# Weight and activation tiles moved to starts on multiples of 128 bytes or more, 260-column weight units in halves

## The chip, the cores and the metric

The kernel runs on one core of a Trainium2 chip, in one launch. The metric is device time in microseconds (us), the median of the runs timed; lower is better. TensorE (PE) does the matmuls, VectorE (DVE) and ScalarE (ACT) the elementwise work, GpSimd (POOL) a few powers and products, and SyncE (SP) issues the transfers. Each of the 128 partitions of the on-chip memory (SBUF) is a row of bytes; a tile takes the same stretch of bytes in every partition, and "address" below means the byte in that row at which a tile or a slice begins.

## The reference, cut to what matters

Two layers on 256 tokens of width 1024, all in float32. `D_FF` is 2816.

```
for l in range(2):
    x = x + 0.5 * swiglu(rmsnorm(x), ffn1_w_in[l], ffn1_w_out[l])
    h = rmsnorm(x)
    x = x + (hybrid_ab_mixer(h) if l == 0 else pool_mixer(h))
    x = x + 0.5 * swiglu(rmsnorm(x), ffn2_w_in[l], ffn2_w_out[l])
return rmsnorm(x)

swiglu(h, w_in, w_out):  gate, up = split(h @ w_in);  (silu(gate) * up) @ w_out
hybrid_ab_mixer(h):      q, k, v, z, b, a, su, sv = split(h @ w_in)
                         # convolution and gated delta rule on q, k, v; gate z; spatial gating of su by sv
                         concat([o_a, o_b]) @ w_out
```

## The kernel before, in words

**Matmuls in three products.** To keep float32 accuracy at the matmul rate of the float32r type, every weight and activation is split into a rounded part `hi` and a remainder `lo`, both float32r. One product of 128 rows then takes three matmuls: hi by hi, hi by lo, lo by hi. Each matmul has a stationary operand of 128 columns, loaded into the array beforehand, and a moving operand whose columns are streamed through it. There are two forms:

- `products_t` (lines 286 to 288): the weights are stationary, the activations of all 256 tokens move. So run the input projections of the FFNs ("pair" units: gate and up for 128 channels; moving `xth`, `xtl`), the q, k and v projections, the output projections of l0a and l0b ("outt" units; moving `hh`, `hl`), and the mixer's output projection (moving `sgh`, `sgl`, `dnh`, `dnl`).
- `products` (lines 278 to 281) and `some` in `out_by_token` (line 437): the activations are stationary, and 512 columns of weights (260 for two units) move from `hi` and `lo`. So run the output projections of l1a and l1b, the first chunk of l1b, and sv, su, ba and z of the mixer; with 256 columns the pool mixer.

**Weights.** They lie packed in one array in the order of use, as units of up to 2080 columns per partition. `load_next` takes a buffer `raw` (3 of them), issues the unit's transfer on SP's queue, and splits it in two halves: ACT writes `hi`, DVE writes `lo` (4 buffers each). `take` hands out the next unit and first calls `load_next` so that loading stays 2 units ahead (1 in the mixer, where a 512-column projection is two units of 4 blocks and a 260-column projection, ba or z, one unit of 8 blocks at a pitch of 260). Within an engine the order of the instructions is fixed when the kernel is built; a planner may put ready work of one part between that of another.

**Where the tiles lie.** A pool lays its tiles one behind the other in order of first use, in multiples of 32 bytes. In the pool `base` these are, with their bytes per partition:

```
xth 8192, xtl 8192, prm 512, xt 8192, ident 512, ones 512, mhalf 64, junk 1024,
raw 3 x 8320, hi 4 x 8320, lo 4 x 8320, sq 2 x 1024, ms 2 x 64, r 2 x 64, rd 1024, rb 2 x 1024, rp 2 x 64, ss 2 x 64
```

The memory map of the built kernel puts `xth` at byte 16512, which is 129 x 128. So `xth`, `xtl` and all up to `mhalf` begin on multiples of 128. `mhalf` takes 64 bytes, and `junk`, `raw`, `hi` and `lo` (8320 is 65 x 128) begin 64 bytes past a multiple of 128. The pools of the stages follow `base`. In the four FFN pools `hh` and `hl` (22528 bytes each) are the first tiles and begin 64 bytes past a multiple of 128 too. In the mixer's pool small tiles of 32 and 64 bytes come first; there `sgh` begins 96 past a multiple of 128, `sgl` on one, `dnh` 96 and `dnl` 32 past one.

`WIDE` (line 27) is the columns of a weight buffer, `LINE` (line 26) those of a small statistics tile. `wide` (line 621) hands out one of two buffers of 4 x 259 values that the mixer uses in turn.

Of the kernel before, what the change touches and what calls it, by code (L numbers as in the profile page):

```python
# [9 lines left out]
F32 = mybir.dt.float32  # L10
F32R = mybir.dt.float32r
# [4 lines left out]
P = 128  # L16
D = 1024
KD = D // P
T = 256
DFF = 2816  # L20
NF = DFF // P
H = 4
# [3 lines left out]
LINE = 16  # L26
WIDE = 130 * LINE
# [26 lines left out]
def weight_units():  # L54

    units = []

    def ffn(name):
        f0 = 0
        if name in FIRST_BY_TOKEN:  # L60
            f0 = 4
            for part in ("g", "u"):
                for h in range(2):
                    units.append((name, "chunk", h, part, 4 * 512))
        for f in range(f0, NF):
            units.append((name, "pair", f, "", 2 * KD * P))
        if name in BY_CHANNEL:
            for d in range(KD):
                for h in range(2):
                    units.append((name, "outt", d, h, NF // 2 * P))  # L70
        else:
            for u in range(NF // 2):
                units.append((name, "out", u, "", 2 * D))

    ffn("l0a")
    for n, w in MIX_CHUNKS:
        halves = 2 if w == 512 else 1
        for h in range(halves):
            units.append(("mix", "in", n, h, KD // halves * w))
    for u in range(4):  # L80
        units.append(("mix", "out", u, "", 2 * D))
    ffn("l0b")
    ffn("l1a")
    units.append(("pool", "w", 0, "", 8 * 256))
    ffn("l1b")
    return units
# [90 lines left out]
def trunk(ctx: ExitStack, tc: tile.TileContext, x_in, xt_in, wts, prm_in, ident_in, mixc_in, band_in,  # L177
          sgw_in, sgn_in, pscale_in, fin_in, out):
    nc = tc.nc
    pe, dve, act, pool = nc.tensor, nc.vector, nc.scalar, nc.gpsimd  # L180

    base = ctx.enter_context(tc.tile_pool(name="base", bufs=1))
    ps = ctx.enter_context(tc.tile_pool(name="ps", bufs=1, space=PSUM))
# [17 lines left out]
    ones = base.tile([P, P], F32, name="ones")  # L201
    pool.memset(ones, 1.0)
    mhalf = base.tile([P, 16], F32, name="mhalf")
# [16 lines left out]
    units = weight_units()  # L220
# [4 lines left out]
    def load_next():  # L225
        u = len(loaded)
        name, kind, _, _, n = units[u]
        raw = base.tile([P, WIDE], F32, tag="raw", name="raw", bufs=RAW_BUFS)
# [4 lines left out]
        if u == 0:  # L233
            for i in range(4):
                c = slice(i * 512, (i + 1) * 512)
                special["first"](i)
                nc.sync.dma_start(out=raw[:, c], in_=src[:, c])
                split(hi[:, c], lo[:, c], raw[:, c])
            return
# [10 lines left out]
        half = n // 2  # L250
# [56 lines left out]
    class Norm:  # L307
# [15 lines left out]
        def means(self):  # L323
            b = chain(0)
            for t in range(2):
                for s in (self.sum, self.last):
                    pe.matmul(out=b[:, t:t + 1], lhsT=s[:, t * P:(t + 1) * P], rhs=ones[:, 0:1],
                              start=s is self.sum, stop=s is self.last)
            ms = base.tile([P, LINE], F32, tag="ms", name="ms", bufs=2)[:, :2]
            dve.tensor_scalar(out=ms, in0=b[:, :2], scalar1=1.0 / D, scalar2=EPS, op0=ALU.mult, op1=ALU.add)  # L330
            r2 = base.tile([P, LINE], F32, tag="r", name="r", bufs=2)[:, :2]
            power(r2, ms)
            self.r = [r2[:, t:t + 1] for t in range(2)]
            self.r2 = r2
# [178 lines left out]
    def rstd(t):  # L513

        ss = base.tile([P, LINE], F32, tag="ss", name="ss", bufs=2)
# [3 lines left out]
        ms = base.tile([P, LINE], F32, tag="ms", name="ms", bufs=2)[:, 0:1]  # L519
# [3 lines left out]
    with tc.tile_pool(name="pl", bufs=1) as pp:  # L523
# [7 lines left out]
        band_r = pp.tile([P, 4, P + 16], F32, name="band_r")  # L531
        x_tail = pp.tile([P, D], F32, name="x_tail")
        last = Norm()
        last.r2 = base.tile([P, LINE], F32, tag="r", name="r", bufs=2)[:, :2]
        last.r = [last.r2[:, t:t + 1] for t in range(2)]

        def pooled(t):
            r = base.tile([P, LINE], F32, tag="rp", name="rp", bufs=2)[:, 0:1]
# [45 lines left out]
    def final(t):  # L584
        o = fin_pool.tile([P, D], F32, tag="o", name="o", bufs=2)
        halves = [slice(n * 512, (n + 1) * 512) for n in range(2)]
        r = base.tile([P, LINE], F32, tag="rp", name="rp", bufs=2)[:, 0:1]
# [11 lines left out]
def mixer(tc, e):  # L599
# [9 lines left out]
    def load(w):  # L609
        if w == 512:  # L610
            return [blocks_of(take("mix", "in", 1), w, 0, 4) for _ in range(2)]
        return [blocks_of(take("mix", "in", 1), w, 0, KD)]

    with tc.tile_pool(name="mx", bufs=1) as mp:
# [6 lines left out]
        def wide(form="p h t -> p h t"):  # L621
            return mp.tile([P, H, T + 3], F32, tag="wide", name="wide", bufs=2).rearrange(form)
# [3 lines left out]

        mixc, sgn, ws = consts["mixc"], consts["sgn"], consts["sgw"]
# [64 lines left out]
        sv = mp.tile([P, 2, 512], F32, tag="sv", name="sv")  # L692
# [5 lines left out]
        def conv(first):  # L698
            y = mp.tile([P, H, T], F32, name=f"y{first}")
            pre = wide()  # L700
# [23 lines left out]
        def norms(y, at):  # L724

            sq = wide()[:, :, :T]
# [111 lines left out]
        raw_sv, sv = sv, wide("p h t -> p (h t)")[:, :1024].rearrange("p (t c) -> p t c", t=2)  # L838
# [12 lines left out]
        su = wide("p h t -> p (h t)")[:, :1024].rearrange("p (t c) -> p t c", t=2)  # L851
# [24 lines left out]
        sg_parts = (mp.tile([P, 4, 2, P], F32R, tag="sv", name="sgh"), mp.tile([P, 4, 2, P], F32R, name="sgl"))  # L876
# [66 lines left out]
        for u in range(2):  # L943
            w = take("mix", "out", 1)
            for i in range(2):
                for d in range(KD):
                    some(OUT_ORDER[2 * u + i], i, w, d)
        dn_parts = tuple(mp.tile([P, H, T + 3], F32R, tag="wide", name=n, bufs=2).rearrange("p h t -> p (h t)")[:, :1024]
                         .rearrange("p (k t c) -> p k t c", k=4, t=2) for n in ("dnh", "dnl"))
# [40 lines left out]
```

## Time and profile before

| | us |
|---|---|
| median of 3 runs | 917.57 |
| lowest and highest | 914.7, 920.32 |
| the profiled execution's own time | 916.53 |
| its span, first to last instruction | 914.7 |

The profile is of one execution. A line of a view names the line of the kernel, the engine, the operation and the tiles as out<-in. A matmul's duration in it covers its passage through the array, which overlaps with the next ones; the pace, from one start to the next, is had by counting matmuls in a stretch. A window counts every instruction that touches it, so a stretch of matmuls without a gap has the pace (length of the window + one duration) / count; one duration is 0.28 us for 256 columns and 0.39 us for 512.

### The profile page before, as it was taken

The page shows a single profiled execution, that of the slowest core. Times are in us where ns is not written, and L with a number is a line of the kernel's source. Part 1 is how long each engine was busy: PE and PEld are TensorE (multiplying, and loading weights), DVE is VectorE, ACT ScalarE, POOL GpSimd, SP SyncE. Part 2 cuts the span into 40 slices and gives each one's busy share as a digit, 9 for nine tenths or more (in the row PEclk, how much of TensorE's full clock was granted, in tenths as well). Part 3 has the DMA queues.
Part 4 walks back from the last instruction along what each step waited for, and adds up shares of the span by engine and source line. Part 5 has one row for each costly group of instructions (what it writes and reads, how often), then busy time and mean ns, then how long its engine had stood idle before and what let it go on. Part 6 is the DMA issues. An engine that isn't in the chain of part 4 may idle for free.

```text
span 914.7 us, 16344 instructions
## 1 busy us (share of the span) xinstructions
PE 897.9 (98%) x6900; PEld 855.1 (93%) x6900; DVE 573.6 (63%) x907; ACT 456.9 (50%) x717; POOL 28.9 (3%) x40
## 2 busy tenths in 40 slices
PE   8999999999999999999999999999999999999996
PEld 7999999999988989999999999999888789999885
DVE  5866656667887676666556666566555566666443
ACT  6655534466647565544444545455335445544331
POOL 0000000000221000000000000000000000000000
PEclk9999999999999999999999999999999899999999
DMA  7865545663224235555455765555555165555521
GB/s 275 336 197 203 168 130 188 218 232 136 96 92 164 72 136 216 198 185 174 153 165 201 265 232 205 172 201 195 184 186 182 48 231 192 199 184 188 193 81 47
DMA packets 25851, 162.86 MB, mean 178 GB/s; under 512 B 2993, under 2 KB 3121, under 8 KB 9649
## 3 DMA queue, kind: packets, MB, share of 16 engines
q1 hardware_dynamic: 25488, 161.29, 51.0%
q8 instruction: 54, 0.88, 0.4%
q10 hardware_dynamic: 288, 0.52, 0.1%
q14 instruction: 21, 0.16, 0.0%
HBM read 160.75 MB, written 1.05 MB: 177 GB/s over the span
## 4 chain that ended last, share of the span: by engine, by line
PE 94%; DVE 3%; ACT 1%; DMA 1%; issue 0%; SPq 0%; POOL 0%; POOLq 0%; ACTq 0%; DVEq 0%
PE mm L286 18%; PE mm L288 18%; PE mm L287 18%; PE acc L437 13%; PE acc L288 5%; PE acc L286 5%; PE acc L287 5%; PE mm L278 2%; PE mm L279 2%; PE mm L281 2%; DMA xt<-in_xt 1%; PE acc L556 1%; PE acc L799 0%; PE acc L793 0%; PE acc L271 0%
## 5 line engine op out<-in xcount | busy, mean ns | idle before, releaser
L213 ACT CAST hi<-raw 128x1024 fp32r<-128x1024 f32 (+2 forms) x318 | 307.0, 986 | 331.7 <-PE mm L287 204.0
L214 DVE TENSOR_TENSOR lo<-raw,hi 128x1024 fp32r<-128x1024 f32 (+2 forms) x318 | 360.7, 1151 | 125.9 <-ACT hi L213 125.4
L286 PE MATMUL mm<-xth,hi 128*128 128x256 f32 x1440 | 400.9, 279 | 0.5 <-ACT xth L216 0.5
L287 PE MATMUL mm<-xtl,hi 128*128 128x256 f32 x1440 | 399.9, 278 | 0.5 <-DVE xtl L217 0.4
L288 PE MATMUL mm<-xth,lo 128*128 128x256 f32 x1440 | 399.1, 277 | 0.8 <-DVE lo L214 0.8
L286 PEld LDWEIGHTS mm<-xth,hi 128*128 128x128 f32 x1440 | 271.0, 188 | 1.5 <-ACT xth L216 0.9
L287 PEld LDWEIGHTS mm<-xtl,hi 128*128 128x128 f32 x1440 | 271.3, 188 | 1.0 <-DVE xtl L217 0.9
L288 PEld LDWEIGHTS mm<-xth,lo 128*128 128x128 f32 x1440 | 271.0, 188 | 1.2 <-DVE lo L214 1.2
L405 DVE TENSOR_TENSOR sg<-mm,rb 128x256 f32<-128x256 f32 x84 | 35.3, 424 | 112.5 <-PE mm L288 112.3
L286 PE MATMUL acc<-hh,hi 128*128 128x256 f32 x352 | 99.3, 282 | 0.0
L288 PE MATMUL acc<-hh,lo 128*128 128x256 f32 x352 | 99.2, 282 | 0.0
L287 PE MATMUL acc<-hl,hi 128*128 128x256 f32 x352 | 99.1, 282 | 0.0
L437 PE MATMUL acc<-hi,hh 128*128 128x512 f32 x176 | 69.3, 394 | 0.0
L437 PE MATMUL acc<-lo,hh 128*128 128x512 f32 x176 | 69.0, 392 | 0.0
L437 PE MATMUL acc<-hi,hl 128*128 128x512 f32 x176 | 69.0, 392 | 0.0
L286 PEld LDWEIGHTS acc<-hh,hi 128*128 128x128 f32 x352 | 66.7, 189 | 0.0
L288 PEld LDWEIGHTS acc<-hh,lo 128*128 128x128 f32 x352 | 66.6, 189 | 0.0
L287 PEld LDWEIGHTS acc<-hl,hi 128*128 128x128 f32 x352 | 66.6, 189 | 0.0
L213 ACT CAST hh<-hid 128x256 fp32r<-128x256 f32 x84 | 34.0, 408 | 27.8 <-DVE hid L408 27.7
L437 PEld LDWEIGHTS acc<-hi,hl 128*128 128x128 f32 x176 | 33.0, 188 | 7.7
L437 PEld LDWEIGHTS acc<-hi,hh 128*128 128x128 f32 x176 | 33.0, 188 | 7.5
L437 PEld LDWEIGHTS acc<-lo,hh 128*128 128x128 f32 x176 | 33.1, 188 | 7.3
(211 smaller groups left out, 784.9 us busy)
## 6 DMA issues: line engine op xcount, KB each, us to landing
raw<-in_wts SPq DMA_DIRECT2D x124, 1024.0 KB, 4.9
raw<-in_wts SPq DMA_DIRECT2D x32, 704.0 KB, 4.1
raw<-in_wts SPq DMA_DIRECT2D x2, 1040.0 KB, 4.9
xt<-in_xt SPq DMA_DIRECT2D x4, 256.0 KB, 5.7
raw<-in_wts SPq DMA_DIRECT2D x4, 256.0 KB, 5.9
mixc<-in_mixc SPq DMA_DIRECT2D x1, 640.0 KB, 6.3
band<-in_band SPq DMA_DIRECT2D x1, 544.0 KB, 6.4
psc<-in_pscale SPq DMA_DIRECT2D x1, 512.0 KB, 8.2
```

Of the source, the lines that this page charges most:

```text
L213: act.copy(out=hi, in_=src)
L214: dve.tensor_tensor(out=lo, in0=src, in1=hi.bitcast(F32), op=ALU.subtract)
L278: pe.matmul(out=b, lhsT=ah, rhs=wh, start=start and i == 0, stop=False)
L279: pe.matmul(out=b, lhsT=ah, rhs=wl, start=False, stop=False)
L281: pe.matmul(out=b, lhsT=al, rhs=wh, start=False, stop=stop and i == n - 1)
L286: pe.matmul(out=b, lhsT=wh, rhs=ah, start=start, stop=False, **more)
L287: pe.matmul(out=b, lhsT=wh, rhs=al, start=False, stop=False, **more)
L288: pe.matmul(out=b, lhsT=wl, rhs=ah, start=False, stop=stop, **more)
L405: dve.tensor_tensor(out=sg, in0=gate, in1=norm.rb, op=ALU.mult)
L437: pe.matmul(out=acc[t][n], lhsT=a, rhs=w[part][:, n * 512:(n + 1) * 512], start=first and i == 0, stop=last and i == 2)
L556: pe.matmul(out=o, lhsT=x[:, t, c], rhs=band_r[:, g, :P], start=True, stop=True)
```

## The change

The tiles that float32r matmuls read get other addresses. Small statistics tiles are made 128 bytes (`LINE` = 32), `mhalf` and the rows `ms`, `r`, `ss` are set out first in `base` (7 tiles of 128 bytes, so `xth` begins at 16512 + 896 = 17408, which is 17 x 1024), and `WIDE` becomes 2048 columns, 8192 bytes. Two tiles `pad` that nothing uses round up what stands before others. In the mixer, both `wide` buffers (now 4 x 264 values, 33 x 128 bytes), `sv` and `sgl` are set out first. Since a unit of 2080 columns no longer fits, ba and z are packed as two units of 4 blocks, like the 512-column projections; each is loaded by one transfer that puts its 260-column blocks at a pitch of 512 columns, and split in two pieces of two blocks, so that each block begins on a multiple of 2048 bytes. No arithmetic changes.

```diff
-LINE = 16
-WIDE = 130 * LINE
+LINE = 32
+WIDE = 2048
...
     for n, w in MIX_CHUNKS:
-        halves = 2 if w == 512 else 1
-        for h in range(halves):
-            units.append(("mix", "in", n, h, KD // halves * w))
+        for h in range(2):
+            units.append(("mix", "in", n, h, KD // 2 * w))
...
     base = ctx.enter_context(tc.tile_pool(name="base", bufs=1))
+    def row(tag):
+        return base.tile([P, LINE], F32, tag=tag, name=tag, bufs=2)
+    mhalf = base.tile([P, LINE], F32, name="mhalf")
+    for tag in ("ms", "r", "ss"):
+        row(tag)
...
     ones = base.tile([P, P], F32, name="ones")
+    base.tile([P, P], F32, name="pad")
     pool.memset(ones, 1.0)
-    mhalf = base.tile([P, 16], F32, name="mhalf")
...
+        if n == 4 * 260:
+            raw, src, hi, lo = (a.rearrange("p (k c) -> p k c", k=4) for a in (raw, src, hi, lo))
+            nc.sync.dma_start(out=raw[:, :, :260], in_=src)
+            for c in (slice(0, 2), slice(2, 4)):
+                split(hi[:, c, :260], lo[:, c, :260], raw[:, c, :260])
+            return
...
         band_r = pp.tile([P, 4, P + 16], F32, name="band_r")
+        pp.tile([P, P], F32, name="pad")
...
     def load(w):
-        if w == 512:
-            return [blocks_of(take("mix", "in", 1), w, 0, 4) for _ in range(2)]
-        return [blocks_of(take("mix", "in", 1), w, 0, KD)]
+        halves = [blocks_of(take("mix", "in", 1), 512, 0, 4) for _ in range(2)]
+        return [[(wh[:, :w], wl[:, :w]) for wh, wl in half] for half in halves]
...
-        def wide(form="p h t -> p h t"):
-            return mp.tile([P, H, T + 3], F32, tag="wide", name="wide", bufs=2).rearrange(form)
+        def wide(name="wide", dtype=F32):
+            return mp.tile([P, H, T + 8], dtype, tag="wide", name=name, bufs=2)
+        def flat(a):
+            return a.rearrange("p h t -> p (h t)")[:, :1024]
...
+        wides = [wide(), wide()]
+        sv = mp.tile([P, 2, 512], F32, tag="sv", name="sv")
+        sgl = mp.tile([P, 4, 2, P], F32R, name="sgl")
...
-            pre = wide()
+            pre = (wides.pop() if wides else wide())[:, :, :T + 3]
...
-            sq = wide()[:, :, :T]
+            sq = (wides.pop() if wides else wide())[:, :, :T]
...
-        sg_parts = (mp.tile([P, 4, 2, P], F32R, tag="sv", name="sgh"), mp.tile([P, 4, 2, P], F32R, name="sgl"))
+        sg_parts = (mp.tile([P, 4, 2, P], F32R, tag="sv", name="sgh"), sgl)
...
-        dn_parts = tuple(mp.tile([P, H, T + 3], F32R, tag="wide", name=n, bufs=2).rearrange("p h t -> p (h t)")[:, :1024]
-                         .rearrange("p (k t c) -> p k t c", k=4, t=2) for n in ("dnh", "dnl"))
+        dn_parts = tuple(flat(wide(n, F32R)).rearrange("p (k t c) -> p k t c", k=4, t=2) for n in ("dnh", "dnl"))
```

What is left out replaces `base.tile([P, LINE], ...)` by `row(...)` and `wide("p h t -> p (h t)")[:, :1024]` by `flat(wide())`.

## Rows read from the trace of the kernel before

**Rows 1.** The page: busy time of each engine, and its granted clock in 40 slices.

```profile
PE 897.9 (98%) x6900; PEld 855.1 (93%) x6900; DVE 573.6 (63%) x907; ACT 456.9 (50%) x717; POOL 28.9 (3%) x40
...
PEclk9999999999999999999999999999999899999999
```

**Rows 2.** The page: the chain of work that ended last, share of the span by engine.

```profile
PE 94%; DVE 3%; ACT 1%; DMA 1%; issue 0%; SPq 0%; POOL 0%; POOLq 0%; ACTq 0%; DVEq 0%
```

**Rows 3.** Windows, PE alone: stretch and length, busy (matmuls), granted clock, DMA share, GB/s.

```profile
40.00:140.00 100.00, 100.00 (x882) 1.00 0.54 183
155.00:195.00 40.00, 40.00 (x339) 1.00 0.63 215
312.00:318.00 6.00, 6.00 (x53) 1.00 0.01 3
...
360.00:480.00 120.00, 120.00 (x1051) 1.00 0.52 177
...
589.00:593.00 4.00, 4.00 (x36) 1.00 0.46 137
596.00:603.00 7.00, 7.00 (x64) 1.00 0.45 154
645.00:695.00 50.00, 50.00 (x218) 1.00 0.55 190
```

**Rows 4.** Groups by line and shape, PE: how many matmuls of each kind.

```profile
L286 PE MATMUL mm<-xth,hi 128*128 128x256 f32 x1440 | 400.9, 279 | 0.5 <-ACT xth L216 0.5
...
L286 PE MATMUL acc<-hh,hi 128*128 128x256 f32 x352 | 99.3, 282 | 0.0
...
L437 PE MATMUL acc<-hi,hh 128*128 128x512 f32 x176 | 69.3, 394 | 0.0
...
L278 PE MATMUL mm<-hi,xth 128*128 128x512 f32 x64 | 25.9, 405 | 1.0 <-ACT xth L213 1.0
```

**Rows 5.** The chain in order of time: start, length, what and how often.

```profile
205.99 0.93 PE mm L281 x4
...
237.41 1.68 PE acc L732 x16
...
246.03 0.59 DVE wide L711
...
257.25 0.45 PE acc L799 x4
...
277.00 0.96 PE mm L281 x8
...
347.18 0.43 PE acc L341 x2
```

**Rows 6.** Groups by line and shape, ACT: the rounding of weights into hi.

```profile
L213 ACT CAST hi<-raw 128x1040 fp32r<-128x1040 f32 x4 | 4.1, 1061 | 5.7 <-PE mm L287 3.9 <-PE acc L287 1.8
...
L213 ACT CAST hi<-raw 128x512 fp32r<-128x512 f32 x4 | 2.4, 605 | 0.2 <-DMA raw<-in_wts 0.2
```

**Rows 7.** Groups by line and shape, DVE: the remainders of weights into lo.

```profile
L214 DVE TENSOR_TENSOR lo<-raw,hi 128x1040 fp32r<-128x1040 f32 x4 | 5.4, 1367 | 1.7 <-ACT hi L213 1.7
...
L214 DVE TENSOR_TENSOR lo<-raw,hi 128x512 fp32r<-128x512 f32 x4 | 2.8, 692 | 0.4 <-ACT hi L213 0.4
```

**Rows 8.** The page, DMA issues: bytes, and median us from issue to landing.

```profile
raw<-in_wts SPq DMA_DIRECT2D x2, 1040.0 KB, 4.9
...
psc<-in_pscale SPq DMA_DIRECT2D x1, 512.0 KB, 8.2
```

**Rows 9.** Timeline of SP near 175 us: the first of the two is ba's transfer.

```profile
175.05 4.19 SPq L240 DMA_DIRECT2D raw<-in_wts  x2
```

**Rows 10.** Timeline of PE near 196 us: the first matmul of ba.

```profile
195.92 0.28 PE L278 MATMUL mm<-hi,xth 128*128 128x260 f32 x1
```

**Rows 11.** Timeline of PE near 275 us: the first matmul of z.

```profile
274.92 0.28 PE L278 MATMUL mm<-hi,xth 128*128 128x260 f32 x1
```

**Rows 12.** Timeline of ACT in the stage of z.

```profile
273.64 3.90 ACT L213 CAST hi<-raw 128x1024 fp32r<-128x1024 f32 x4 [4.03 <-PE mm L287]
```

More of the change, by code (lines that the diff above doesn't have):

```diff
@@ L328, in means @@
                               start=s is self.sum, stop=s is self.last)
-            ms = base.tile([P, LINE], F32, tag="ms", name="ms", bufs=2)[:, :2]
+            ms = row("ms")[:, :2]
             dve.tensor_scalar(out=ms, in0=b[:, :2], scalar1=1.0 / D, scalar2=EPS, op0=ALU.mult, op1=ALU.add)
-            r2 = base.tile([P, LINE], F32, tag="r", name="r", bufs=2)[:, :2]
+            r2 = row("r")[:, :2]
             power(r2, ms)
@@ L513, in rstd @@
     def rstd(t):
-        ss = base.tile([P, LINE], F32, tag="ss", name="ss", bufs=2)
+        ss = row("ss")
         for n in range(2):
@@ L518, in rstd @@
                            accum_out=ss[:, n:n + 1])
-        ms = base.tile([P, LINE], F32, tag="ms", name="ms", bufs=2)[:, 0:1]
+        ms = row("ms")[:, 0:1]
         dve.tensor_scalar(out=ms, in0=ss[:, 0:1], scalar1=ss[:, 1:2], scalar2=EPS, op0=ALU.add, op1=ALU.add)
@@ L531, in trunk @@
         band_r = pp.tile([P, 4, P + 16], F32, name="band_r")
+        pp.tile([P, P], F32, name="pad")
         x_tail = pp.tile([P, D], F32, name="x_tail")
         last = Norm()
-        last.r2 = base.tile([P, LINE], F32, tag="r", name="r", bufs=2)[:, :2]
+        last.r2 = row("r")[:, :2]
         last.r = [last.r2[:, t:t + 1] for t in range(2)]
         def pooled(t):
-            r = base.tile([P, LINE], F32, tag="rp", name="rp", bufs=2)[:, 0:1]
+            r = row("rp")[:, 0:1]
             power(r, rstd(t))
@@ L586, in final @@
         halves = [slice(n * 512, (n + 1) * 512) for n in range(2)]
-        r = base.tile([P, LINE], F32, tag="rp", name="rp", bufs=2)[:, 0:1]
+        r = row("rp")[:, 0:1]
         power(r, rstd(t))
@@ L689, in mixer @@
             dl.append(c)
-        sv = mp.tile([P, 2, 512], F32, tag="sv", name="sv")
         banks = project(512, load(512), False)
@@ L835, in mixer @@
             act.activation(out=zs[:, t, 252:], in_=banks[t][:, :260], func=AF.Silu, scale=r[t])
-        raw_sv, sv = sv, wide("p h t -> p (h t)")[:, :1024].rearrange("p (t c) -> p t c", t=2)
+        raw_sv, sv = sv, flat(wide()).rearrange("p (t c) -> p t c", t=2)
         act.activation(out=sv, in_=raw_sv, func=AF.Gelu)
@@ L850, in mixer @@
                                          op0=ALU.mult, op1=ALU.mult)
-        su = wide("p h t -> p (h t)")[:, :1024].rearrange("p (t c) -> p t c", t=2)
+        su = flat(wide()).rearrange("p (t c) -> p t c", t=2)
         banks = project(512, load(512), False)
```

## The prediction

> **What bounds the kernel now.** I read the page first. TensorE is busy for 98% of the span and the others for 63% or less [rows 1], and the chain of work that ended last lies on PE for 94% of the time [rows 2]. So the end moves by what a matmul costs, and hardly by what ACT, DVE or the transfers cost. The granted clock is at full speed, 2.4 GHz, in nearly every slice [rows 1] and 1.00 in every stretch used below [rows 3], so the clock explains none of the differences.
>
> Next I read windows that hold nothing but matmuls, and took the pace (window plus one duration, over the count). Matmuls of 256 moving columns come in two paces. In the pair stages, where `xth` and `xtl` move, it is 100.28 / 882 = 113.7 ns and 120.28 / 1051 = 114.4 ns; in the outt stage, where `hh` and `hl` move, 40.28 / 339 = 118.8 ns; in the mixer's output projection 6.28 / 53 = 118.5 ns [rows 3]. Count, shape, clock and stationary operand (`hi` and `lo`, 64 bytes past a multiple of 128) are the same in all three. What differs is the address of the moving operand: on a multiple of 128 for `xth` and `xtl`, 64 past one for `hh` and `hl`, mostly off one in the mixer. With 512 moving columns of `hi` or `lo`, 64 past a multiple, the pace is 50.39 / 218 = 231.1 ns [rows 3], and 0.93 / 4 = 232 ns in the mixer [rows 5]. Twice 113.7 would be 227.4. The last two come with a stationary operand off (L437, `hh`) and on a multiple of 128 (L281, `xtl`), and are alike: for 512 columns the stationary address doesn't tell, the moving one may.
>
> The reading is not clean. Between 589 and 593 us the pair stage itself runs at 4.28 / 36 = 118.9 ns, and between 596 and 603 us, with the same moving tiles, at 7.28 / 64 = 113.8 ns [rows 3]. And in the stretch from 312 us one of three matmuls moves `sgl`, which is on a multiple of 128, yet the whole stretch is at 118.5. So an aligned moving tile can reach 113.7 but need not, and the tiles off a multiple do not reach it in any stretch that I read.
>
> **The change part by part.** After it the float32r tiles, moving and stationary, begin on multiples of 128 bytes (the sizes add up so: 896 bytes of small tiles ahead of `xth`, weight buffers of 8192, `wide` of 4224).
>
> (a) outt: 3 x 352 = 1056 matmuls [rows 4] go from 118.8 to 113.7 ns: 1056 x 5.1 = 5.4 us.
>
> (b) 512 moving columns: 3 x 176 = 528 of L437 and 3 x 64 = 192 of L278 to L281 [rows 4]. The trace has no 512-column float32r matmul on a multiple of 128, so its pace is bounded: at best 0.43 / 2 = 215 ns, which two passes of 256 float32 columns take [rows 5] and which is nearly 512 columns at 2.4 GHz (213 ns); at worst 227 ns, twice the aligned 256. I take the middle, 221: 528 x 10.1 = 5.3 us and 192 x 11 = 2.1 us. The ends give 11.8 and 3.1 us in all in place of 7.4.
>
> (c) 260 columns: 2 projections x 2 token tiles x 8 blocks x 3 = 96 matmuls from 0.96 / 8 = 120 ns [rows 5] to 113.7 x 260 / 256 = 115.5: 0.4 us.
>
> (d) The mixer's output projection (4 units x 2 x 8 x 3 = 192) and the pool mixer's 48: 240 x 5 = 1.2 us.
>
> (e) The pair stages stay at their pace: 0. If the slow stretches in them go as well, about (114.4 - 113.7) ns over 4320 matmuls, 3 us at most.
>
> All of (a) to (d) stand on the path, since PE has no gaps in these stretches: 5.4 + 7.4 + 0.4 + 1.2 = 14.4 us. Faster matmuls ask for weights sooner. A unit of 24 matmuls of 512 columns would last 5.3 us in place of 5.5; its splitting takes about 2 x 1.4 us on DVE [rows 7], and its transfer lands in 4.9 us with three buffers in turn [rows 8]. PE stays the bound.
>
> What the halves of ba and z cost: four casts of 520 columns in place of two of 1040. By the 512-column rows that is 4 x 0.61 - 2 x 1.06 = 0.3 us of ACT and 4 x 0.70 - 2 x 1.37 = 0.1 us of DVE per unit [rows 6, 7], beside PE. Two transfers in runs of 1040 bytes take the place of one in runs of 8320. No row has that form; two halves of one 4.9 us transfer would cost nothing, and two like psc's 8.2 us would land 11.5 us later [rows 8]. ba's transfer starts at 175.05 and its first matmul at 195.92 [rows 9, 10]: 21 us less 4.9 is more than 11.5. I take zero, on either end.
>
> Both projections fill one more of the four `hi` and `lo` buffers, so the unit four places on is split one place later. For su's first half this cover is thin: its buffer comes free with q's last matmul, at about 274.9 [rows 11], z lasts 48 x 120 ns = 5.8 us, and two casts and the last subtraction take 2 x 1.06 + 1.37 = 3.5 us; 2.3 us are spare. ACT does take up casts at once when such buffers come free, four in a row [rows 12]. The price if ACT or DVE is held up elsewhere is up to 3.5 us, there and once more at sv after ba. Behind a waiting cast stand ACT's silu of z and its square of q's convolution, which PE needs only after z. The planner may also mix the mixer's pieces in another order. I take 0.3 us for all of it, bounds -1 and +3.
>
> The swapped turns of `wide`: v's convolution now writes the buffer of k's squares instead of k's inputs. PE has read the squares by 239.1 and DVE writes v's first half at 246.03 [rows 5]; 7 us of cover, zero cost, 7 us later the most that its loss could bring. Longer small rows and pads: zero, they are storage.
>
> Sum: 14.4 - 0.3 = 14.1 us. The profiled execution took 916.53 us, 1.0 below the median, with a span of 914.7; from it, 916.5 - 14.1 = 902.4. I forecast 902. The case's own range, from the ends of (b), (e) and the mixer, is 894 to 909.
>
> **The rivals.**
>
> Slower: the address of the moving operand against that of the weights decides, not either one alone. While one matmul streams, PE loads the weights of the next. In the pair stage the two lie 64 bytes apart modulo 128, and this is the one relation seen at 113.7; in outt both are 64 past, relation zero, and slow. After the change the relation is zero everywhere. Then the pair and q, k, v matmuls, 3 x 1440 = 4320 [rows 4], fall to the outt pace: 4320 x 5.1 = 22.0 us lost, nothing won in (a), 916.5 + 22.0 + 0.3 = 939; with the 7.4 us of (b), 931. It decides from the point at which more than two thirds of the pair matmuls lose their pace. Two pair stretches on the same tiles at two paces speak for some such interplay; against it, the 512-column rows show no gain when the weights are on a multiple and the moving tile 64 past, which is also 64 apart. Chance 0.20.
>
> No change: the start of a tile does not matter, and the 113.7 belongs to `xth` for another reason, or is a phase that the stage falls into by itself (589 to 603 us). Then the time is 916.5 + 0.3 = 917. The Trainium skill speaks for it: "SBUF — State Buffer", section Specifications (TRN2), gives the memory lines of 16 bytes and a penalty for crossing to a new one. By that rule a start 64 bytes past a multiple of 128 is as good as one on it, and the sum is zero. The trace disagrees as far as 118.8 against 113.7 goes. Chance 0.14.
>
> Faster still: the weight loads gain too. Matmuls of 128 float32 columns, whose streams are short, come every 0.45 / 4 = 112.5 ns [rows 5], which I take for the pace that loading 128 weight columns allows. From 113.7 to 112.5 over 4320 + 1056 + 240 matmuls is 6.7 us, and 512 columns at 215 give 4.4 more: 891. Chance 0.10. The Trainium skill, "TensorE: Matmul & The Clock Gate", section Back-to-back issue gap, gives N / 2.4 + 2.5 ns for an isolated matmul: 109.2 and 215.8 ns. No stretch here shows 109.2 for float32r; by an estimate from that page the pair stages alone would give 4320 x 4.5 = 19 us.
>
> **How the numbers follow.** Main case 0.56, slower 0.20, no change 0.14, faster still 0.10. The predicted time is the main case's. Within 1% (908.4 to 926.7; three runs spread over 0.6%, so less is hard to tell from nothing) lie the no-change case and 0.03 of the main one, 0.17. Below lie 0.53 + 0.10 = 0.63, above 0.20. The range 888 to 932 holds the first, third and fourth cases and the milder part of the second; the rest, some 0.15, is left out.
>
> **What would show it.** In the profile after, windows inside outt should hold about 355 matmuls in 40 us in place of 339, windows of L437 about 228 in 50 us in place of 218, pair windows 882 in 100 us as before. If pair windows hold 845, the slower rival is right. If 339 and 218 stay, nothing came of the addresses. If PE shows gaps between 270 and 285 us, the halves cost more than I gave. What would make it wrong most easily is the pair stage: it holds 4320 of the matmuls, it has its pace already, and I cannot show that it keeps it once the weights move too.

## The result, and the profile after

The kernel after takes 942.26 us (median of 6 runs, 938.92 to 945.36), the kernel before 917.79 (6 runs, 914.70 to 920.32). The ratio is 1.0264, 95% interval 1.0232 to 1.0295: slower, where 902 was forecast. Products stand at lines 300 to 302 (`products_t`), 292 to 295 (`products`) and 451 (`out_by_token`) in the kernel after; the splits of weights at 220 and 221.

The page of the kernel after, against [rows 1, 2, 8]: busy times with the granted clock, the chain by engine, and the transfers of the halves (count, KB each, us to landing).

```profile
PE 918.9 (98%) x6900; PEld 879.6 (94%) x6900; DVE 574.0 (61%) x911; ACT 456.7 (49%) x721; POOL 30.0 (3%) x40
...
PEclk9999999999999999999999999999999999999999
...
PE 92%; DVE 4%; ACT 1%; DMA 1%; issue 1%; POOL 1%; SPq 0%; POOLq 0%; ACTq 0%
...
raw<-in_wts SPq DMA_DIRECT2D x4, 520.0 KB, 4.1
```

TensorE (PE) is the bound as before, with the same 6900 matmuls, a granted clock of 0.9 or more in every slice (1.00, that is 2.4 GHz, in every stretch used below), and 21 us more busy time. So each matmul costs more. The windows say which, PE alone (stretch and length, busy with the count, granted clock, DMA share, GB/s), against [rows 3]; the stretches after 195 us are set later, since the stages begin later. l0a, l0b, l1a and l1b are the two FFNs of layer 0 and of layer 1, in order.

```profile
40.00:140.00 100.00, 100.00 (x836) 1.00 0.52 177
155.00:195.00 40.00, 40.00 (x336) 1.00 0.58 184
319.00:325.00 6.00, 6.00 (x52) 1.00 0.01 3
365.00:465.00 100.00, 100.00 (x835) 1.00 0.51 174
...
560.00:650.00 90.00, 90.00 (x754) 1.00 0.51 176
596.00:603.00 7.00, 7.00 (x61) 1.00 0.42 150
665.00:715.00 50.00, 50.00 (x222) 1.00 0.57 193
```

The pace is again (window + one duration) / count. Where a pace is said to be "from start to start", it is the mean step between the starts of neighbouring matmuls in the trace, without gaps. Pairs take 100.28 / 836 = 119.95 ns (before 113.7), 120.1 in l0b (before 114.4) and 119.7 in l1a. The outt stage takes 40.28 / 336 = 119.9 (before 118.8), the mixer's last product 6.28 / 52 = 120.8 (118.5); there one matmul is 2.3 ns, and from start to start it is 119.3 (118.6). The 512-column streams of l1a take 50.39 / 222 = 227.0 (before 231.1). All matmuls of 256 columns have come to one pace, 120 ns; in the trace 5308 of 5529 of them start exactly 120 ns before the next.

The groups by line and shape of the kernel after, against [rows 4, 6, 7], show that the counts are unchanged and what the halves of ba and z cost in splitting.

```profile
L300 PE MATMUL mm<-xth,hi 128*128 128x256 f32 x1440 | 409.6, 285 | 2.5 <-ACT hi L220 1.5 <-ACT xth L223 1.1
...
L451 PE MATMUL acc<-hi,hh 128*128 128x512 f32 x176 | 68.6, 390 | 0.0
...
L220 ACT CAST hi<-raw 128x520 fp32r<-128x520 f32 x8 | 4.6, 625 | 10.0 <-PE mm L301 5.4 <-PE acc L301 4.6
...
L221 DVE TENSOR_TENSOR lo<-raw,hi 128x520 fp32r<-128x520 f32 x8 | 6.4, 825 | 1.3 <-ACT hi L220 1.3
```

ba's two transfers in the timeline of SP, and the first matmuls of ba and of z in that of PE, against [rows 9 to 11]:

```profile
182.16 4.41 SPq L250 DMA_DIRECT2D raw<-in_wts  x2
...
203.21 0.28 PE L292 MATMUL mm<-hi,xth 128*128 128x260 f32 x1
...
281.81 0.28 PE L292 MATMUL mm<-hi,xth 128*128 128x260 f32 x1
```

From ba to z it is 78.6 us, 79.0 before, and from ba to l0b's first matmul 137.2, 137.4 before: the mixer did not get slower by the halves or by the swapped turns of `wide`. The loss lies in the stages that run on `products_t`. By these paces: pairs and q, k, v 4320 x (120.0 - 114.0) = +25.9 us, outt 1056 x 1.1 = +1.2, the mixer's output 192 x 0.8 = +0.1, streams 528 x 4.1 + 192 x 3.5 = -2.8 (L278 to L281 went from 232 to 228.5 from start to start). That is +24.4; the spans differ by 22.4, the medians by 24.5.

### The profile page after: what moved, and what is told of

It is laid out like the page before. It is cut to its first block, busy times and chain, and to the rows that moved or that the text cites. A ratio compares the mean times of both kernels' runs of the same rounds, so it can differ in the third digit from the quotient of the medians.

```text
span 937.1 us, 16363 instructions
## 1 busy us (share of the span) xinstructions
PE 918.9 (98%) x6900; PEld 879.6 (94%) x6900; DVE 574.0 (61%) x911; ACT 456.7 (49%) x721; POOL 30.0 (3%) x40
## 4 chain that ended last, share of the span: by engine, by line
PE 92%; DVE 4%; ACT 1%; DMA 1%; issue 1%; POOL 1%; SPq 0%; POOLq 0%; ACTq 0%
PE mm L300 19%; PE mm L302 19%; PE mm L301 19%; PE acc L451 12%; PE acc L302 5%; PE acc L300 5%; PE acc L301 5%; PE mm L292 2%; PE mm L293 2%; PE mm L295 1%; DVE lo L221 1%; DMA xt<-in_xt 1%; PE acc L571 1%; DVE y L737 0%; ACT hi L220 0%
## 5 line engine op out<-in xcount | busy, mean ns | idle before, releaser
L220 ACT CAST hi<-raw 128x1024 fp32r<-128x1024 f32 (+3 forms) x322 | 307.3, 976 | 357.8 <-PE mm L301 230.4
L221 DVE TENSOR_TENSOR lo<-raw,hi 128x1024 fp32r<-128x1024 f32 (+3 forms) x322 | 360.6, 1137 | 125.7 <-ACT hi L220 125.3
L300 PE MATMUL mm<-xth,hi 128*128 128x256 f32 x1440 | 409.6, 285 | 2.5 <-ACT hi L220 1.5
L302 PE MATMUL mm<-xth,lo 128*128 128x256 f32 x1440 | 408.0, 283 | 1.0 <-DVE lo L221 1.0
L301 PE MATMUL mm<-xtl,hi 128*128 128x256 f32 x1440 | 408.1, 284 | 0.5 <-DVE xtl L224 0.4
L300 PEld LDWEIGHTS mm<-xth,hi 128*128 128x128 f32 x1440 | 276.2, 192 | 3.9 <-ACT hi L220 2.1
L302 PEld LDWEIGHTS mm<-xth,lo 128*128 128x128 f32 x1440 | 276.2, 192 | 1.4 <-DVE lo L221 1.4
L301 PEld LDWEIGHTS mm<-xtl,hi 128*128 128x128 f32 x1440 | 276.2, 192 | 1.0 <-DVE xtl L224 0.9
L419 DVE TENSOR_TENSOR sg<-mm,rb 128x256 f32<-128x256 f32 x84 | 35.4, 424 | 137.4 <-PE mm L302 137.3
```

The source lines that it names most:

```text
L220: act.copy(out=hi, in_=src)
L221: dve.tensor_tensor(out=lo, in0=src, in1=hi.bitcast(F32), op=ALU.subtract)
L300: pe.matmul(out=b, lhsT=wh, rhs=ah, start=start, stop=False, **more)
L301: pe.matmul(out=b, lhsT=wh, rhs=al, start=False, stop=False, **more)
L302: pe.matmul(out=b, lhsT=wl, rhs=ah, start=False, stop=stop, **more)
L419: dve.tensor_tensor(out=sg, in0=gate, in1=norm.rb, op=ALU.mult)
```

## Experiments

The theories of the first four kernels. R: what counts is the distance, modulo 128, of the address of the streamed operand from that of the loaded one; zero is slow for 256 columns. W: the weights' own address; on a multiple of 128 they are slow. M: the streamed operand has to be on a multiple of 128 and the weights off it. S: the halves of ba and z, or the order of the mixer, not the addresses. All edits are to the kernel after, save in the fourth. "Pair", "outt" and "stream" paces below are from windows of PE in the stages of l0a, l0a and l1a.

The ratio is to runs of before that were timed along with each kernel (their medians lie between 916.57 and 918.05 us).

| kernel | weights, activations (mod 128) | us | ratio to before, 95% | pair, outt, stream ns |
|---|---|---|---|---|
| before | 64; 0, hh and hl 64 | 917.79 | | 113.4, 118.8, 231.1 |
| after | 0; 0 | 942.26 | 1.0264 (1.0232 to 1.0295) | 120.1, 119.9, 227.0 |
| e1 | 64; 0 | 918.79 | 1.0005 (0.9981 to 1.0029) | 113.4, 117.6, 233.3 |
| e2 | 0; 64 | 930.84 | 1.0139 (1.0108 to 1.0169) | 117.7, 117.9, 234.4 |
| e3 | 96, 0, 32, 64 in turn; 0 | 928.86, one run | | 117.4, 117.3, 231.1 |
| e4 | as before | 915.63 | 0.9974 (0.9957 to 0.9992) | 113.3, 118.8, 231.1 |
| e8 | 32; 0 | 941.21, one run | | 118.3, 120.1, 234.4 |
| e10 | 64; 64 | 943.46, one run | | 119.9, 119.8, 227.0 |
| e12 | 64; 0, l1's hh and hl 64 | 919.93 | 1.0029 (1.0014 to 1.0044) | 113.3, 117.6, 232.2 |
| e14 | 64, low parts 128 further; 0 | 911.80 | 0.9942 (0.9923 to 0.9961) | 113.4, 113.2, 231.1 |
| e15 | 0, low parts 128 further; 64 | 920.28 | 1.0038 (1.0015 to 1.0062) | 113.4, 113.2, 230.1 |
| e9 | by use (below); 0 | 910.01 | 0.9912 (0.9894 to 0.9931) | 113.3, 113.5, 230.1 |
| e11 | by use, streams 0 mod 256; 0 | 909.16 | 0.9906 (0.9886 to 0.9925) | 113.4, 113.2, 226.0 |
| e13 | as e11, with q, k, v | 908.72 | 0.9906 (0.9882 to 0.9929) | 113.4, 113.2, 226.0 |

The windows: 40 to 130 us for pairs (90.28 over the count), 145 to 190 for outt (45.28), 50 us inside l1a's output projection for the streams (50.39); before's and after's outt and streams are those of the sections above. One matmul more or less in a window is 0.2, 0.3 and 1 ns.

**e1: weights 64 past, activations on multiples.**

```diff
     junk = base.tile([P, 512], mybir.dt.bfloat16, name="junk")
+    base.tile([P, 16], F32, name="shift")
...
         load_next()
+        base.tile([P, 16], F32, name="back")
```

> The changed kernel with all weight buffers (raw, hi, lo) moved 64 bytes up, so that they begin 64 past a multiple of 128 as in the kernel before, while xth, xtl, hh, hl, sgh, sgl, dnh and dnl stay on multiples. Theory R (the moving address against the weights' address modulo 128 decides; 64 apart is fast, zero apart slow): pair and outt stages both at 113.4 ns in place of 120.0, so 4320 x 6.6 + 1056 x 6.6 = 35 us less than the changed kernel: 907, 1.2% below the kernel before. Theory W (the weights' own address decides, 64 past is fast): the same 907, so this run does not tell R from W. Theory S (the halves of ba and z and the new order of the mixer cost the time): 942 as the changed kernel.

918.79 us: 64 bytes ahead of the weight buffers give back the whole loss. Windows of e1, PE: pairs of l0a, outt, pairs of l0b.

```profile
40.00:130.00 90.00, 90.00 (x796) 1.00 0.56 190
145.00:190.00 45.00, 45.00 (x385) 1.00 0.59 188
365.00:445.00 80.00, 80.00 (x708) 1.00 0.54 186
```

Pairs are at 113.4 again, as in before. But outt, with `hh` and `hl` on multiples and the weights 64 past, as R and M want it, stays at 45.28 / 385 = 117.6.

**e2: the reverse, activations 64 past, weights on multiples.**

```diff
+    base.tile([P, 16], F32, name="shift")
     xth = base.tile([P, KD, 2, P], F32R, name="xth")
...
-    base.tile([P, P], F32, name="pad")
+    base.tile([P, P - 16], F32, name="pad")
...
         load_next()
+        base.tile([P, 16], F32, name="shift2")
```

> The mirror image: the weights stay on multiples of 128 as in the changed kernel, and all activations (xth, xtl, hh, hl, sgh, sgl, dnh, dnl) begin 64 past one. Theory R: 64 apart again, pair and outt at 113.4 ns, about 907. Theory W: the weights are on multiples, so pair and outt stay at 120.0: about 942. A third theory, M (a moving operand must be on a multiple and the weights off it), gives 942 as well. For 512 moving columns no theory has a number: 226.7 ns (both on multiples) and 231 (both 64 past) are known.

930.84 us, between the two. Windows of e2: pairs of l0a, and of l1a before 580 us and after 589.

```profile
40.00:130.00 90.00, 90.00 (x767) 1.00 0.55 189
...
553.00:580.00 27.00, 27.00 (x232) 1.00 0.54 193
...
589.00:630.00 41.00, 41.00 (x364) 1.00 0.56 193
```

117.7 ns, 27.28 / 232 = 117.6, and then 41.28 / 364 = 113.4 on the same tiles. W and M fall in their strict form: 113.4 is reached with the weights on multiples and the streamed tiles off them. R stands for the zero distance, but says too little: 64 apart has two paces, 113.3 and about 117.7. The change falls where four transposes by `by_token` stand between pair units, the first at 581.9 us.

**e3: four places in turn.** Weight buffers of 2056 columns, so that units begin 96, 0, 32 and 64 past.

```diff
-WIDE = 2048
+WIDE = 2048 + 8
...
-            raw, src, hi, lo = (a.rearrange("p (k c) -> p k c", k=4) for a in (raw, src, hi, lo))
+            raw, src, hi, lo = (a[:, :w].rearrange("p (k c) -> p k c", k=4) for a, w in ((raw, 2048), (src, n), (hi, 2048), (lo, 2048)))
...
+        base.tile([P, 8], F32, name="back")
```

> The changed kernel with weight buffers at a pitch of 8224 bytes, so that the four of hi, and the four of lo alike, begin 96, 0, 32 and 64 bytes past a multiple of 128, unit by unit in turn; all activations on multiples. Theory R and W: in the pair and outt stages every fourth unit (64) at 113.4 ns and every fourth (0) at 120.0; 32 and 96 are open: as slow as 0 if only 64 is special, in between if the distance counts. If the pace depends on what the stage fell into before, units of one offset will differ among themselves.

Windows of e3 in l0a: the first inside a unit 96 past, the second inside one 64 past, then such a pair once more.

```profile
58.50:63.00 4.50, 4.50 (x41) 1.00 0.48 178
64.20:68.50 4.30, 4.30 (x40) 1.00 0.43 179
81.00:85.50 4.50, 4.50 (x41) 1.00 0.54 180
86.50:91.00 4.50, 4.50 (x42) 1.00 0.45 189
```

4.78 / 41 = 116.6 and 4.58 / 40 = 114.5 by these short windows; from start to start it is 118.2 and 113.3. The units on a multiple or 32 past run at 118 to 119. Only 64 apart shows 113.3.

**e4: before, with the halves of ba and z alone.**

```diff
-        halves = 2 if w == 512 else 1
-        for h in range(halves):
-            units.append(("mix", "in", n, h, KD // halves * w))
+        for h in range(2):
+            units.append(("mix", "in", n, h, KD // 2 * w))
...
+        if n == 4 * 260:
+            raw, src, hi, lo = (a[:, :w].rearrange("p (k c) -> p k c", k=4) for a, w in ((raw, 2048), (src, n), (hi, 2048), (lo, 2048)))
+            nc.sync.dma_start(out=raw[:, :, :260], in_=src)
```

(and in `load`, as in the change.)

> The kernel before with the second part of the change alone: ba and z as two units each at a pitch of 512 columns, all tiles where they were. Theories R and W: 917 to 920, no difference (the mixer was 137.5 us from ba's first matmul to l0b's first in the kernel before and 137.2 in the changed one, with 250 matmuls slowed in it). Theory S: most of the 24.5 us, 935 or more.

915.63 us, 0.9974 of before: S is out, the halves cost nothing and perhaps win 1 to 4 us by the interval. Where, the profiles do not settle: the profiled execution of e4 has a span of 916.0, at a mean granted clock of 0.990 for before's 0.993. From ba to z it took 77.5 us for before's 79.0, but from ba to l0b's first matmul 137.4 as in before.

The next four sharpen R to D: zero apart leaves 120 for 256 columns and gives 227 for 512; 64 apart allows 113.3 and 117.8, one of which goes on until a gap draws again. N is the rival without such a rule.

**e5: placing by use, first try.** Units that are loaded (`products_t`) 64 past, units that are streamed on multiples.

```diff
+        held = kind in ("pair", "outt") or name == "mix" and (kind == "out" or units[u][2] in CONV_CHUNKS)
+        o = 16 * (held ^ u % 2)
-        hi = base.tile([P, WIDE], F32R, tag="hi", name="hi", bufs=SPLIT_BUFS)
+        hi = base.tile([P, WIDE + 16], F32R, tag="hi", name="hi", bufs=SPLIT_BUFS)[:, o:o + WIDE]
```

(`lo` likewise.)

> The kernel after, with each weight unit placed by how it is used: units that are loaded as weights (pairs, outt, k, v, q and the mixer's last product) begin 64 bytes past a multiple of 128, units that are streamed (chunk, out, sv, su, ba, z, pool) on a multiple; the activations stay on multiples. Theory D (the distance of the streamed address from the loaded one modulo 128 sets the pace; zero leaves 256 columns only 120 ns, 64 apart allows 113.3 and 117.8; 512 columns go the other way, zero 227 and 64 apart 232): 702 matmuls of 512 columns go from the 232.3 ns of the kernel with weights 64 past to 227.1, so its 918.8 us less 3.7, 915; and 910.5 if outt (1056 matmuls) draws the faster of its two paces this time, 113.3 for 117.8. So 910 to 916. Rival N (it is the weights' own addresses, or where all buffers stand together, and no rule by use): the times of the kernels with all weights at one place, 918 or more, with outt at 117.8 and the streams at 231 to 233.

919.94 us (ratio 1.0027, 1.0013 to 1.0040), above D's range; the time is within N's, but outt is at 115.4 from start to start and the streams at 229.6, where N has 117.8 and 231 to 233. The kernel was not what it meant to be: the addresses show `hi` and `lo` of one unit in buffers of different number, so that in half of the units one of the two is on the wrong side. The units with both 64 past ran at 113.3 to 113.4 from start to start, in outt too; the other pair units had means of 115 to 118.

**e6: high parts 64 past, low parts on multiples** (`hi` 32 columns longer and begun 16 columns in).

> The kernel after, with the high parts of the weights 64 bytes past a multiple of 128 and the low parts on multiples; activations on multiples. Of each three matmuls the first two have the high part loaded, the third the low part. Theory D with the matmul's own weights: the interval from the third matmul to the next is 120, those from the first two 113 or 118. If it is the weights that are being loaded meanwhile for the next matmul: the interval from the second is 120 and the other two are short. Rival N: all three alike, at 120 or at a mean between. Device time by D 925 to 932 (a third of 5500 matmuls at 120, two thirds at 113.3 to 117.8), by N 930 to 942.

934.19 us (one run), above D's 925 to 932 and inside N's range; pairs at 90.28 / 767 = 117.7. From start to start in l0a the first matmul of three takes 116.7, the second 117.4, the third, with the low part loaded, 119.2. That leans to the matmul's own weights, but no class is at 113 or 120: a mixed sequence has a mixed pace. It doesn't settle which load counts.

**e7: e2 with transposes between pair units.** They are extra work; their result is not used.

```diff
+                if f > 1 and not (fill and f in fill):
+                    b = chain(0)
+                    for i in range(4):
+                        pe.transpose(out=b[:, i * P:(i + 1) * P], in_=xt[:, i, 0, :], identity=ident)
```

> The kernel with activations 64 bytes past and weights on multiples, with four transposes of a stored tile into a chain bank after the pair units from the third on wherever there are none (their result is not used; the outputs are the same). Theory D: at 64 apart there are two paces, 113.3 and 117.8, and one goes on until a gap draws again; so pair units of all stages change between the two from unit to unit, and over a quarter of the 48 or so units after a gap run at 113 to 114, where without the transposes only the last units of one stage did. Rival N (the places of that one stage's tiles): the pair units stay at 117.8 except in the stage of layer 1's first block. The transposes themselves cost about 1 us a unit at most.

956.19 us with the added work. Windows of e7: pairs of l0a, of l0b, of l1a before and after the transposes at 558.5 us, of l1b.

```profile
40.00:130.00 90.00, 90.00 (x797) 1.00 0.52 178
365.00:445.00 80.00, 80.00 (x685) 1.00 0.50 172
553.00:558.00 5.00, 5.00 (x45) 1.00 0.46 170
...
570.00:630.00 60.00, 60.00 (x532) 1.00 0.52 183
790.00:835.00 45.00, 45.00 (x387) 1.00 0.48 164
```

l0a is at 113.3 from the first added transposes at 31.7 us on (before them, and in e2, 117.8), and l1a from 559 us on at 60.28 / 532 = 113.3; that is against N. l0b and l1b, with the same transposes after every unit, stayed at 117 with the transposes counted in, 117.8 from start to start between them. So such a gap can end the slower pace and mostly does not, and in e7 no stage went back from 113.3. "Draws again" at every gap was wrong.

**e8: all weights 32 past** (as e1, with 8 and 24 columns).

> The kernel after with all weight buffers 32 bytes past a multiple of 128, activations on multiples. Theory D, narrow form (113.3 only at 64 apart, as the kernel with four places let see): pairs and outt at 118 to 119, 512 columns at 231 to 233, device time 932 to 938. Wide form (any distance but zero admits 113.3): some stages at 113.3, time under 930. Rival N: as after, 120 throughout, 940 or more.

941.21 us, pairs 118.3, outt 120.1, streams 234.4. No stage shows 113.3, as the narrow form says, but outt is no better than in after and the streams are worse, so the time is above its 932 to 938.

**e9: placing by use, even buffers.** `WIDE + 32` and `o = 16 * held` in e5, one spare tile of 512 bytes taken out.

> The placing by use again, now as it was meant: in the first attempt the high and the low part of a unit didn't come from buffers of the same number, so that in half of the units one of the two stood on the wrong side. Here every buffer is 128 bytes longer and all begin on multiples (a spare tile of 512 bytes makes room), and units that are loaded as weights start 64 bytes in, streamed units at the start. Theory D: 256 columns at 113.3 or 117.8, 512 columns at 227.1, so 910 to 916 as worked out for the first attempt. Rival N (no rule by use): 918 or more, 512 columns at 230 or more.

**e10: both 64 past** (e2 with a tile of 64 bytes after `junk` and none after the first `load_next`).

> The kernel after with both the weight buffers and all activations that TensorE reads 64 bytes past a multiple of 128. Theory D (their distance counts, and it is zero again): 256 columns at 120 in the pair stages, 512 columns near 227, device time 938 to 943 as after. Rival K (what costs is that one of the two stands on a multiple of 128, or that both do): 256 columns at 118 or below, 512 columns at 231 or more, 918 to 931.

Windows of e9 (pairs, outt), then of e10 (pairs, outt, streams):

```profile
40.00:130.00 90.00, 90.00 (x797) 1.00 0.56 190
145.00:190.00 45.00, 45.00 (x399) 1.00 0.61 196
```

```profile
40.00:130.00 90.00, 90.00 (x753) 1.00 0.55 183
145.00:190.00 45.00, 45.00 (x378) 1.00 0.54 174
...
669.00:719.00 50.00, 50.00 (x222) 1.00 0.55 189
```

e10 repeats the kernel after (119.9, 119.8, 227.0; 943.46 us, half a us above D's range) with no tile of the float32r matmuls on a multiple of 128: it is the distance, and K is out. e9 comes to 910.01 us, 0.9912 of before, faster than both kernels. But not by the sum it was given: outt fell to 113.5, the streams stayed at 230.1. Half of its buffers lie 128 past a multiple of 256, and the streams tell that apart.

**e11: by use, streams on multiples of 256.**

```diff
+        hi, lo = (base.tile([P, WIDE + 32], F32R, tag=f"{part}{u % SPLIT_BUFS}", name=part, bufs=1)[:, o:o + WIDE]
+                  for part, o in (("hi", 16 * held), ("lo", 16 if held else 32)))
```

> The placing by use with the streamed weights on multiples of 256 (each of the eight buffers has a place of its own; streamed low parts start 128 bytes in, since their buffers begin 128 past a multiple of 256). In the placing by use before it 512 columns took 230.8 ns and not 227.1: every second buffer stood 128 past a multiple of 256, and the stationary tiles on one. Theory D with 256 in place of 128 for the streams: 512 columns at 227, 702 x 3.8 = 2.7 us less than 910.0, so 907; 256 columns at 113.3 to 117.8 as before. If the 128 bytes don't matter and something else holds the streams at 230.8: 910.

**e12: e1 with `hh` and `hl` of l1a and l1b 64 past.**

```diff
+            if name not in BY_CHANNEL:
+                fp.tile([P, 16], F32, name="shift")
             hh = fp.tile([P, NF, 2, P], F32R, name="hh")
```

> The kernel with all weights 64 bytes past a multiple of 128 and activations on multiples, but hh and hl of the two blocks whose output weights are streamed (l1a, l1b) also 64 past, so that only there the distance is zero. Theory D: the 524 matmuls of the output projections of these blocks go from 233.3 to 227 ns, 3.3 us; pairs as before at 113.3: 918.8 less 3.3, 915.5, or 911 if outt draws the faster of its paces. Rival N: 918 to 919, the streams at 233.

The streams' windows of e11 and of e12:

```profile
639.00:689.00 50.00, 50.00 (x223) 1.00 0.56 193
```

```profile
645.00:695.00 50.00, 50.00 (x217) 1.00 0.54 188
```

e11's streams are at 50.39 / 223 = 226.0 (226.8 from start to start), as expected; the time, 909.16, is below that of e9 by 0.9 where 2.7 was expected, and the intervals overlap. e12's are at 232.2, and its time is not better than e1's; N's 918 to 919 came nearer than D's 915.5. Its `hh` came to lie 192 past a multiple of 256 and the weights 64: apart by 128, not zero. I had reckoned modulo 128 there; with 256 both runs fit, and so does e9.

The profiled execution of e12 shows one thing more. The pair tiles of l1b lie as in e1, yet they ran at 80.28 / 682 = 117.7 where e1 had 80.28 / 709 = 113.2, some 3.8 us over the stage. So the same addresses gave either pace. The windows in l1b's pairs, of e12 and then of e1:

```profile
760.00:840.00 80.00, 80.00 (x682) 1.00 0.55 190
```

```profile
760.00:840.00 80.00, 80.00 (x709) 1.00 0.56 189
```

**e13: e11 with k, v and q 64 past too**, which a slip in the name list had left out of e5, e9 and e11 (`CONV_CHUNKS = ("k", "v", "q")` for the numbers 2 to 4).

> In the three placings by use so far k, v and q were still on multiples by a slip in the list of units (their 289 matmuls ran at 119 to 120). Here they are 64 past as well, all else as in the placing with the streams on multiples of 256. Theory D: 289 x 6.3 = 1.8 us less than 909.2, so 907 to 908. Rival (these projections wait for something else): 909.

Windows in q, k, v of e11, and of e13:

```profile
221.00:239.00 18.00, 18.00 (x154) 1.00 0.37 119
```

```profile
219.00:237.00 18.00, 18.00 (x162) 1.00 0.39 119
```

18.28 / 154 = 118.7 (with short matmuls among them) against 112.8; from start to start the stage is at 119.8 against 114.3. The pace is D's; the 1.8 us are too few to be seen in 908.72 (904.60 to 911.93) against 909.16.

**e14 and e15: e1 and e2 with 128 bytes between the high and the low buffers.**

```diff
+        if u == 0:
+            base.tile([P, 32], F32, name="gap")
         lo = base.tile([P, WIDE], F32R, tag="lo", name="lo", bufs=SPLIT_BUFS)
```

> The kernel with all weights 64 bytes past a multiple of 128, and 128 bytes of nothing between the high buffers and the low ones, so that modulo 256 the high parts lie 64 and the low parts 192 from the activations. Theory G: with 64 apart the slower pace, 117.8, lasts only where all three matmuls of a group have the same distance modulo 256; with 64 and 192 in turn it passes into 113.3. So outt goes from 117.8 to 113.3 and all 5455 matmuls of 256 columns from 114.64 to about 113.4, 6.8 us less than 918.8: 912. Rival H (which of the two paces a stage gets is chance, or comes from the stage before): outt at 117.8 as without the gap, about 919.

> The kernel with all activations 64 bytes past and weights on multiples, and the same 128 bytes between the high and the low buffers. Without them its pairs ran mostly at 117.8 (mean of 256 columns 117.25, 930.8 us). Theory G: 113.4 in all pair and outt stages, 5471 x 3.85 = 21 us less: 910. Rival H: 117.8 in most stages again, 928 to 933.

Windows of e14: outt; pairs of l0b. Windows of e15: pairs of l0a, outt, pairs of l0b.

```profile
145.00:190.00 45.00, 45.00 (x400) 1.00 0.61 198
365.00:445.00 80.00, 80.00 (x709) 1.00 0.53 183
```

```profile
40.00:130.00 90.00, 90.00 (x796) 1.00 0.56 190
145.00:190.00 45.00, 45.00 (x400) 1.00 0.62 202
365.00:445.00 80.00, 80.00 (x675) 1.00 0.52 174
```

e14 does what G says: outt 113.2 for e1's 117.6, 911.80 us for the 912 expected. That the time fits to 0.2 us is partly luck: the 512-column streams went from 233.3 to 230.4 from start to start, 528 x 2.9 = 1.5 us that G's sum did not have. e15 wins 10.6 us over e2, not 21: l0a, outt and l1 run at 113 to 114, but l0b's pairs stayed at 80.28 / 675 = 118.9 in the profiled execution (914.40 us), and its nine runs spread from 914.40 to 925.65. So high and low parts 128 apart make the faster pace the common one and don't force it.

## Why the prediction was wrong

**The step that failed.** "On a multiple of 128 for `xth` and `xtl`, 64 past one for `hh` and `hl`": I put the two paces of 256 columns down to the streamed operand's own address, although two operands had an address, and in before the distance of the two changed together with it. From this came (e), "the pair stages stay at their pace: 0", which was 25.9 us, and the sign of (a). The rival "the address of the moving operand against that of the weights decides" named the mechanism, put 0.20 on it, and its 939 (without the gain of (b)) is 3 us from the result. That it came so near is in part chance: it counted a loss of 5.1 ns per pair matmul where about 6 were lost, and left out the 2.8 us that (b) did gain. e1 and e10 are the test that was missing: move the weights alone and the loss is gone (918.79), move both and it is back (943.46).

**The objection that misled me.** Against that rival I held that 512 columns show no gain when the weights are 64 apart from the stationary tile. That was so, and is no objection: for 512 columns the order is the reverse. Zero apart modulo 256 they take 226 to 227 (after, e10, e11, e13), else 229 to 234 (all others). What is best for a short stream is not best for a long one.

**Term by term.** (a) Forecast 113.7 in outt, measured 119.9; it does reach 113.2 to 113.5 in e9, e11, e13, e14 and e15, where the distance is 64. (b) Sign right, size at the bad end: 221 taken, 227 the bound, 227.0 measured; worth 2.8 us for 7.4. (c) 115.5 forecast; z's chain in the kernel after shows them at 118:

```profile
282.92 0.47 PE mm L295 x4
```

(d) went the wrong way, 118.6 to 119.3 from start to start. (e) 25.9 us for 0. The halves: 0.3 us taken, -1 to +3 the bounds; e4 measured them alone at -2.4 us by its ratio, -3.9 to -0.7, below the lower bound though the interval reaches into it. The casts took 0.63 where 0.61 was used, and ba's first transfer was issued 21 us ahead of its first matmul and such transfers land in 4.1 us: the covers held. That ACT, DVE and transfers would not matter was right throughout; so was the reading of the bound.

**The row that warned.** In [rows 3] the pair stage of before ran at 118.9 (117.8 from start to start) and then, on the same tiles, at 113.8. That is the pair of paces at 64 apart which e2 and e7 show (117.7 and 113.3). The outt pace of before, 118.8, is close to the slower one, so that "slow" had two causes that the numbers of before hardly tell apart: zero distance (119.9) and the slow pace at 64 (117.6). Nor was before's outt all at zero: its weight buffers of 65 x 128 bytes lie 0 and 128 from `hh` in turn, modulo 256, and 208 of the 528 steps in l0a's outt are exactly 120 ns, with a mean of 119.0 over all.

**The no-change rival.** The Trainium skill, "SBUF — State Buffer", section Specifications (TRN2), with its 16-byte lines, was cited for it: 64 bytes are four whole lines. The runs disagree: 64 bytes ahead of the weights alone are 942.26 against 918.79 us.

**What stays open.** Why zero apart is slow was not shown; a clash of the two reads of TensorE would fit, and is only argued. The Trainium skill, "SBUF — State Buffer", section A bandwidth-pool intuition that's wrong (but worth ruling out), gives the weight loads a second, independent read port; no run here shows the ports. What puts a stage at 64 apart into 113.3 or 117.7 is shown in part (e14, and e15 but for one stage). The side may count too, which no run tested: by the tile sizes, the streamed address less the loaded one, modulo 256, is 192 in e1's pair stages (113.4) and 64 in its outt (117.6) and in e2's pairs (mostly 117.7). It does not decide alone: e12's last pair stage has 192 and ran at 117.7, e7's l0a has 64 and ran at 113.3. Whether a matmul's own loaded operand counts or that of the next, e6 left undecided.

## What to carry to other kernels

Where TensorE bounds a kernel, the addresses of its two operands are read together: of two tiles that a matmul loads and streams, note the distance modulo 128 and 256, and try 64 bytes of padding on one side alone before moving both. "Rounder" starts are no gain in themselves; here they took the best distance from 4320 matmuls to give it to 720, and placing each unit by its use (e11, e13) turned 2.6% lost into 0.9% won (0.3% of it is there with the halves of ba and z alone, by e4). When two explanations of a pace differ only in which operand's address counts, the profile of one layout can't tell them apart, and the number at stake has to be weighed with both.

## What was not expected of the hardware

- 256 float32r columns from start to start, at a granted clock of 1.00 (2.4 GHz): 120 ns with the two operands zero apart modulo 256 (after, e10), a mean of 119.0 where they are 0 and 128 apart in turn (outt of before), 113.3 or 117.7 at 64 apart modulo 128 (118.9 once, l0b of e15), 118 to 120 at 32 (e8).
- 512 columns: 226 to 227 ns zero apart modulo 256 (after, e10, e11, e13), 229 to 234 at 32 (e8), 64 (e1, e2) and 128 (e12) or where distances mix (before, e9, e14).
- The two paces at 64 apart keep themselves up: a stage of 1000 matmuls stays at 117.7 across twenty gaps of four transposes (e7, l0b), another goes over to 113.3 after one (e7, l1a), and the same layout gave 113.2 in one kernel and 117.7 in another (l1b of e1 and e12). The faster pace is not kept for good either: the pair stage of before left it for some 4 us [rows 3].
